# A transformer block on one core: transposes before scaling, 256-byte buffer pitches, later gate sums and 128-row rotary scores

## The chip, the core and the metric

The kernel runs on one core of a Trainium2 chip. Its engines work side by side: TensorE (PE) multiplies matrices, and loads its stationary operands with instructions of their own (PEld); VectorE (DVE) and ScalarE (ACT) do elementwise work; GpSimd (POOL) and SyncE (SP) here mostly issue DMAs. Each engine takes its instructions in order, and waits on semaphores for the others. Operands lie in on-chip memory (SBUF), 128 partitions; a matmul writes to one of eight banks of accumulators (PSUM).

The metric is the device time of one execution in microseconds (us). TensorE's clock is granted by a throttle: 1.00 is full speed.

## What is computed

One layer of a hybrid backbone block, for 256 latent tokens and 256 context tokens of width 2048, all in fp32:

```python
h  = rmsnorm(x, g_attn) * (1 + sc1) + sh1          # and hc from the context tokens
cq, ckv, kr, qn, kn, vn, f = split_columns(h @ w_in)
o_mla = blocked_attention(q_m, cat(k_m, k_mc), cat(v_m, v_mc), MLA_SCALE)   # 8 heads, 128 + 64 rotary
o_na  = neighborhood_attention(...)                # 4 heads
o_fn  = fourier_mix(f, w_fnet)
x  = x + gt1 * (cat(o_mla, o_na, o_fn) @ w_out)
h2 = rmsnorm(x, g_ffn) * (1 + sc2) + sh2
x  = x + gt2 * conv_ffn(h2, w_up, conv_w, conv_b, w_down)
return rmsnorm(x, g_final)
```

The six vectors sh1, sc1, gt1, sh2, sc2, gt2 are silu(c) times a matrix of 2048 x 12288, plus a bias; the context tokens have their own sh1 and sc1.

## The kernel before

**Limbs.** An fp32 operand is held as two numbers of the faster type float32r: a high limb H, and L = value - H. A product of two such operands is three matmuls (`mm3`, lines 108 to 112): H by H, H by L, L by H. Weights come from HBM as raw fp32 tiles of up to 128 x 2048 (SP's queue, `emit_dma`), and `split` makes their limbs: ACT copies to H (line 123), DVE subtracts (line 124). `take(key, i)` (line 181) hands out quarter i of a weight tile and makes limbs ahead of use by `look` quarters, into six `hl` buffers of 4096 bytes per partition.

**Buffers.** Tiles of a tag share that tag's buffers, each as large as the tag's largest tile; tags lie one behind the other. `b8` has 16 buffers. Its largest tile is `h2`, [128, 2, 4, 258] fp32, so the pitch is 8256 bytes; `hx`, `hc`, `act`, `mix`, `hn`, `xT` and the raw weights, of 8192 bytes, lie in it too. `wm2` (4 buffers of 4096 bytes), `acc` (3), `hl` (6), `b1` and `b2` are other tags.

**Stages.** The work on PE, in order:

1. Start. The four tiles of x and context (128 tokens each) are loaded; ACT squares and sums each (line 299), `rstd` gives the inverse root (DVE, POOL), DVE scales x (line 301), and 64 transposes with the identity matrix from `small` turn them into `xT` (line 364).
2. First stage, sixteen rounds. Round g computes sh1 and sc1 for 128 columns (`mod1_mm`, 16 fp32 matmuls of 32 columns of the array, line 318, on 2 MB of `wm1`), transposes the result and makes `hx` and `hc`, the limbs of h (`mod1_h`). `g1` multiplies 128 rows of h by seven column tiles of `wA`, one round behind: four tiles ahead of `mod1_h` and three after it (G1_CUT).
3. V, B and neighbourhood attention, Fourier mixing, latent attention. `mla_scores` makes 128 x 512 scores per head and block: three matmuls on 128 rows, and three on the 64 rotary rows of that head.
4. `wo_unit`: the output projection, then x2, its transposes and h2.
5. Up projection: the first eight pairs on h2 with 258 columns (`up_mm`), the others on `hn` (`up_mm2`, lines 834 and 835: H by H and L in one matmul of 512 columns taken from two places, then L by H with 256 columns). Down projection in four chunks on `act`.

**The other modulation vectors.** The 128 tiles of `wm2` (512 KB each, POOL's queue) are streamed beside all this. `paced` counts matmul columns and calls `fill` at a rate per stage (RATES): one sum that is due, one accumulation on DVE (lines 234 and 236, 128 x 1024), three tiles behind the load (M2_LAG), and one more load. After sixteen tiles a block ends; a gate block's sum is split into limbs, and at the next `fill` PE sums it over the partitions (lines 270 and 271).

The scheduler that lays out each engine's order follows the program, but may pull ready work forward; `tc.issue_after(ins)` holds instructions behind `ins` on its engine.

Of the kernel before, what the change touches and what calls it, by code (L numbers as in the profile page):

```python
# [25 lines left out]
M2_LAG = 3  # L26
CQ_AT = (3, 4, 5)
N_A, G1_CUT = 7, 4
# [4 lines left out]
LOOK_O = 4  # L33
RATES = dict(V=0.647, B=0.336, NA=0.237, F=0.135, FN=0.464, MLA=0.292, O=0.226, UP=0.132, DN=0.428)
# [18 lines left out]
def block_kernel(ctx: ExitStack, tc: tile.TileContext, a, out):  # L53
# [13 lines left out]
    def b8(shape, dt=F32, s="b8"):  # L67
        return sp.tile(shape, dt, tag="b8", bufs=16, name=nm(s))
# [27 lines left out]
    dve.memset(mhalf, -0.5)  # L96
    cs = sp.tile([P, KT, 32], F32, tag="acc", bufs=3, name="cs")
# [10 lines left out]
    def mm3(ps, lH, lL, rH, rL, first, last, skip=False):  # L108
        pe.matmul(ps, lH, rH, start=first, stop=False, skip_group_check=skip)  # L109
        pe.matmul(ps, lH, rL, start=False, stop=False, skip_group_check=skip)  # L110
        pe.matmul(ps, lL, rH, start=False, stop=last, skip_group_check=skip)  # L111
        paced(3 * rH.shape[-1])

# [48 lines left out]
    def quarter(key):  # L162
        if key in kept:
            return b8([P, 2, 512], F32R, s="hk")
        return sp.tile([P, 2, 512], F32R, tag="hl", bufs=6, name=nm("hl"))

    def emit_dma(upto):
        while st[0] <= min(upto, len(order) - 1):
# [4 lines left out]
            last_dma[0] = sync.dma_start(raw[:, :w], a[name][idx]).ins  # L173
# [6 lines left out]

    def take(key, i):

        n = quarters.index((key, i))
        while st[1] <= min(n + look[0], len(quarters) - 1):
            k, q = quarters[st[1]]
            if st[1] > n and order[order.index(k) - 1][0] == "m" and q == 0:
                break
            emit_dma(order.index(k) + ahead[0])
            o, hs = (896 * (q // 2) + 512 * (q % 2), 512 - 128 * (q % 2)) if k[0] == "A" else (
                q * src[k[0]][1] // 4, src[k[0]][1] // 4)  # L190
            t = quarter(k)
# [17 lines left out]
    m2 = {"dma": 0, "acc": 0, "t": {}, "due": None}  # L209
# [31 lines left out]
    def m2_end(blk, acc):  # L241

        if KIND[blk // 2] != "g":
            m2["due"] = (blk, acc)
            return
        lim = []
        for h in range(2):
            hl = sp.tile([P, 2, 512], F32R, tag="acc", bufs=3, name=nm("acl"))
            split(hl[:, 0, :], hl[:, 1, :], acc[:, h * 512 : (h + 1) * 512])
            lim.append(hl)  # L250
        m2["due"] = (blk, lim)

    def m2_sum():
        if m2["due"] is None:
# [13 lines left out]
        for h in range(2):  # L268
            ps = bank()
            pe.matmul(ps, ones_r, v[h][:, 0, :], start=True, stop=False)  # L270
            pe.matmul(ps, ones_r, v[h][:, 1, :], start=False, stop=True)
# [9 lines left out]
    def fill_to(n):  # L281
        while m2["acc"] < n or m2["due"]:
            fill()


    xT = [b8([P, 4, 512], s="xT") for _ in range(4)]
    ssx = const.tile([P, 4], F32, name="ssx")
    rx = const.tile([P, 4], F32, name="rx")
    xt = []
    for t in range(4):  # L290
        x_ = b8([P, D], s="x")
        sync.dma_start(x_, (a["x"] if t < 2 else a["ctx"])[(t % 2) * P : (t % 2 + 1) * P, :])
        xt.append(x_)
        if t == 0:
            act.dma_start(sm, a["small"])
    act.dma_start(rope, a["rope"])
    for t in range(4):
        junk = b8([P, D], s="junk")
        act.activation(junk, xt[t], AF.Square, accum_out=ssx[:, t : t + 1])
        rstd(rx[:, t : t + 1], ssx[:, t : t + 1], D)  # L300
        dve.tensor_scalar(xt[t], xt[t], rx[:, t : t + 1], None, ALU.mult)
    act.activation(c1, smv("c1"), AF.Silu)
# [8 lines left out]
    def mod1_mm(g):  # L311

        for q in range(2):
            w = raw_tile(("m", g, q), 6)
            w = w.rearrange("p (k n) -> p k n", k=8)
            for k in range(8):
                r = 32 * (k % 4)
                pe.matmul(ms[r : r + 32, 0:256], cs[:, 8 * q + k, :], w[:, k, :], start=(q == 0 and k < 4),  # L318
                          stop=(q == 1 and k >= 4), tile_position=(0, r))
        sb = b1(s="part")  # L320
        act.copy(sb, ms[:, 0:256])
        return sb

    def mod1_h(kt, sb):
        for s in range(2):
            pe.transpose(ms[:, 256 + s * P : 256 + (s + 1) * P], sb[:, s * P : (s + 1) * P], ident)
        t = tiny(4, "mt")
        tv = t.rearrange("p (s j) -> p s j", s=2)
        quarters_ = ms[:, 256:512].rearrange("p (s r c) -> p s c r", s=2, r=4)[:, :, 0:2, :]
        dve.tensor_reduce(tv, quarters_, AX.X, ALU.add)  # L330
        dve.tensor_tensor(tv, tv, bm1[:, kt], ALU.add)
        dve.scalar_tensor_tensor(tv[:, 1], tv[:, 1], 1.0, ga[:, kt], ALU.add, ALU.mult)
        m = kt // 4
        if hx[m] is None:
            hx[m] = b8([P, 2, 4, SEQ], F32R, s="hx")
            hc[m] = b8([P, 2, 4, SEQ], F32R, s="hc")
        for j, hh in enumerate((hx, hc)):
# [4 lines left out]
            dve.tensor_scalar(h32, xs, A, B, ALU.mult, ALU.add)  # L342
# [704 lines left out]
```

## Time and profile before

| | us |
|---|---|
| three runs | 1276.1, 1278.97, 1280.82; median 1278.97 |
| profiled execution: device time | 1279.01 |
| its span, first to last instruction | 1277.2 |
| PE, DVE, ACT busy | 1243.7, 978.6, 699.0 |
| mean granted clock | 0.997 |

A row of the profile gives the line, engine and operation of an instruction, its tiles as out<-in, and its shape; in the order of time it begins with start and duration, and ends with the idle time before it and what ended that. Matmuls are pipelined: one of 512 columns lasts 0.39 us and the next starts 0.23 us after it. So for PE the steps from start to start are read, not the durations. PEld overlaps PE.

### The profile page before, as it was taken

How to read it: one execution, taken by the hardware profiler on the slowest of the kernel's cores; microseconds unless marked ns; L12 is line 12 of the kernel's file. 1: busy time of each engine (PE TensorE's matmuls, PEld its weight loads, DVE VectorE, ACT ScalarE, POOL GpSimd, SP SyncE). 2: the span in 40 equal slices, each digit the busy share in tenths (PEclk: the TensorE clock that was granted, in tenths of full speed). 3: DMA queues.
4: the chain of work that ended last, by engine and by line, in shares of the span. 5: the costliest groups of instructions: out<-in, count | busy, mean ns of one | idle time of the engine just before them, and what ended most of it. 6: DMA issues, size and time to landing. Idle time of an engine off the chain costs nothing.

```text
span 1277.2 us, 19956 instructions
## 1 busy us (share of the span) xinstructions
PE 1243.7 (97%) x7536; PEld 1069.2 (84%) x7536; DVE 978.6 (77%) x1757; ACT 699.0 (55%) x1343; POOL 111.5 (9%) x177
## 2 busy tenths in 40 slices
PE   5999999999999999999999999999999999999996
PEld 4888879898787888999988878888888888888885
DVE  5444588999989788899989975777766677777785
ACT  5333323765555555576666544666654566556663
POOL 0000121111111002200121500000000000000000
PEclk9999999999999999999999999999999999999999
DMA  9998689677756977754767857544455645564531
GB/s 387 419 397 327 223 305 323 231 243 249 258 194 232 368 294 270 261 227 165 286 226 253 320 204 264 212 162 169 165 198 180 249 165 183 184 227 165 172 125 66
DMA packets 53648, 304.81 MB, mean 239 GB/s; under 512 B 6064, under 2 KB 7216, under 8 KB 26800
## 3 DMA queue, kind: packets, MB, share of 16 engines
q1 hardware_dynamic: 34256, 234.37, 49.7%
q0 software_dynamic: 18432, 67.12, 15.5%
q10 hardware_dynamic: 864, 2.05, 0.4%
q8 instruction: 59, 0.97, 0.3%
q14 instruction: 37, 0.30, 0.1%
HBM read 301.42 MB, written 2.10 MB: 238 GB/s over the span
## 4 chain that ended last, share of the span: by engine, by line
PE 90%; DMA 3%; DVE 3%; issue 1%; ACT 1%; POOL 0%; DVEq 0%; ACTq 0%; POOLq 0%
PE ps L834 21%; PE ps L109 16%; PE ps L110 15%; PE ps L111 15%; PE ps L835 11%; DMA wm<-in_wm_dram 3%; PE g L109 2%; PE ms L318 2%; PE g L110 2%; PE g L111 2%; DVE acc L236 1%; DVE hl L124 1%; PE ps L493 1%; PE ps L364 1%; DMA sm<-in_small_dram 1%
## 5 line engine op out<-in xcount | busy, mean ns | idle before, releaser
L123 ACT CAST hl<-raw 128x512 fp32r<-128x512 f32 (+2 forms) x732 | 444.0, 611 | 359.8 <-PE ps L111 191.1
L124 DVE TENSOR_TENSOR hl<-raw,hl 128x512 fp32r<-128x512 f32 (+2 forms) x732 | 485.8, 677 | 172.6 <-ACT hl L123 166.4
L834 PE MATMUL ps<-hn,hl 128*128 128x512 f32 x1152 | 404.3, 395 | 0.0
L835 PE MATMUL ps<-hn,hl 128*128 128x256 f32 x1152 | 323.4, 281 | 0.0
L834 PEld LDWEIGHTS ps<-hn,hl 128*128 128x128 f32 x1152 | 216.4, 188 | 51.2
L835 PEld LDWEIGHTS ps<-hn,hl 128*128 128x128 f32 x1152 | 217.1, 188 | 0.2
L236 DVE SCALAR_TENSOR_TENSOR acc<-wm,c,acc 128x1024 f32<-128x1024 f32 x120 | 153.6, 1280 | 8.7 <-DMA wm<-in_wm_dram 8.4
L110 PE MATMUL ps<-hl,act 128*128 128x512 f32 x344 | 135.7, 394 | 0.5 <-DVE hl L124 0.5
L109 PE MATMUL ps<-hl,act 128*128 128x512 f32 x344 | 135.2, 393 | 0.0
L111 PE MATMUL ps<-hl,act 128*128 128x512 f32 x344 | 135.2, 393 | 0.0
L221 POOL DMA_DIRECT2D wm<-in_wm_dram x128 | 68.3, 534 | 310.7 <-DVE acc L236 233.8
L110 PEld LDWEIGHTS ps<-hl,act 128*128 128x128 f32 x344 | 64.7, 188 | 15.9 <-DVE hl L124 1.5
L109 PEld LDWEIGHTS ps<-hl,act 128*128 128x128 f32 x344 | 64.6, 188 | 14.9
L111 PEld LDWEIGHTS ps<-hl,act 128*128 128x128 f32 x344 | 64.7, 188 | 14.6
L109 PE MATMUL ps<-h,hl 128*128 128x258 f32 x256 | 72.5, 283 | 0.0
L111 PE MATMUL ps<-h,hl 128*128 128x258 f32 x256 | 72.1, 282 | 0.0
L110 PE MATMUL ps<-h,hl 128*128 128x258 f32 x256 | 72.1, 282 | 0.0
L216 POOL COPY hold<-hl 128x1 f32<-128x1 f32 x36 | 36.0, 999 | 286.7 <-DVE hl L124 286.7
L109 PE MATMUL ps<-hl,mix 128*128 128x512 f32 x128 | 50.5, 394 | 0.0
L110 PE MATMUL ps<-hl,mix 128*128 128x512 f32 x128 | 50.1, 391 | 0.0
L111 PE MATMUL ps<-hl,mix 128*128 128x512 f32 x128 | 49.9, 390 | 0.0
L855 ACT ACTIVATE cv<-ps,sm 128x256 f32<-128x256 f32 x88 | 49.4, 564 | 0.5
(282 smaller groups left out, 2143.2 us busy)
## 6 DMA issues: line engine op xcount, KB each, us to landing
raw<-in_wup_dram SPq DMA_DIRECT2D x88, 1024.0 KB, 5.1
wm<-in_wm_dram POOLq DMA_DIRECT2D x128, 512.0 KB, 5.1
raw<-in_wdn_dram SPq DMA_DIRECT2D x44, 1024.0 KB, 4.9
raw<-in_wm_dram SPq DMA_DIRECT2D x32, 1024.0 KB, 14.4
raw<-in_wo_dram SPq DMA_DIRECT2D x16, 1024.0 KB, 9.9
raw<-in_wB_dram SPq DMA_DIRECT2D x10, 1024.0 KB, 7.4
raw<-in_wA_dram SPq DMA_DIRECT2D x8, 896.0 KB, 14.5
x<-in_x_dram SPq DMA_DIRECT2D x4, 1024.0 KB, 8.8
```

Of the source, the lines that this page charges most:

```text
L109: pe.matmul(ps, lH, rH, start=first, stop=False, skip_group_check=skip)
L110: pe.matmul(ps, lH, rL, start=False, stop=False, skip_group_check=skip)
L111: pe.matmul(ps, lL, rH, start=False, stop=last, skip_group_check=skip)
L123: act.copy(H, src)
L124: return dve.tensor_tensor(L, src, H.bitcast(F32), ALU.subtract).ins
L216: hold = pool.tensor_copy(tiny(1, "hold"), recent[0][:, 1, 0:1].bitcast(F32)).ins
L221: pool.dma_start(w, a["wm2"][blk * 16 + kt])
L236: dve.scalar_tensor_tensor(m2["a"], w, c1[:, kt : kt + 1], m2["a"], ALU.mult, ALU.add)
L318: pe.matmul(ms[r : r + 32, 0:256], cs[:, 8 * q + k, :], w[:, k, :], start=(q == 0 and k < 4), stop=(q == 1 and k >= 4), tile_position=(0, r))
L834: pe.matmul(ps, w[:, 0, k * P : (k + 1) * P], h[:, :, k, :], start=kt == 0, stop=False, skip_group_check=True)
L835: pe.matmul(ps[:, :SEQ], w[:, 1, k * P : (k + 1) * P], h[:, 0, k, :], start=False, stop=kt == KT - 1, skip_group_check=True)
L855: act.activation(t, ps[:, :SEQ], AF.Identity, bias=c[:, 3:4], scale=c[:, 1:2])
```

## The change

Seven things:

- Transposes work on unscaled x, half a tile at a time, with an identity matrix `idt` that POOL makes; the inverse roots are spread to all partitions as `rxb` by one matmul, and each `mod1_h` multiplies its 128 x 512 of `xT` by it. The x tiles are loaded in halves, the first round's weights between them, `small` and `rope` later.
- In the first stage `a_limbs` makes the limbs of `wA` one round ahead of `g1`, with orders fixed by `issue_after`; G1_CUT is 2. From round 5 on (M2_FROM) fills run there too, at the rate A; the rates V, B and NA are lower.
- Limbs are made 1024 columns at a time, into three buffers of 8192 bytes; `up_mm` goes by halves.
- A gate sum comes SUM_LAG = 6 fills later, except where `fill_to` asks for it at once.
- `qr_limbs` puts H of a head's 64 rotary rows into one half of the partitions and L into the other; scores use two matmuls on 128 rows against krH and krL, which hold the rotary key twice.
- `h8`, four buffers with a pitch of 8448 bytes, takes x, hx, h2, M, f, kh and some of `act`; `b8` has twelve, with a pitch of 8192. h2 has rows of 264 elements; `hn` holds H and L of a row side by side, so line 834's operand is 512 adjoining columns.
- The constants grow by 512 bytes (`idt`).

```diff
-N_A, G1_CUT = 7, 4
+SUM_LAG = 6
+N_A, G1_CUT = 7, 2
-LOOK_O = 4
-RATES = dict(V=0.647, B=0.336, NA=0.237, F=0.135, ...)
+M2_FROM = 5
+LOOK_O = 3
+RATES = dict(A=0.18, V=0.55, B=0.3, NA=0.21, F=0.135, ...)
...
     def b8(shape, dt=F32, s="b8"):
-        return sp.tile(shape, dt, tag="b8", bufs=16, name=nm(s))
+        return sp.tile(shape, dt, tag="b8", bufs=12, name=nm(s))
+    def h8(shape, dt=F32, s="h8"):
+        return sp.tile(shape, dt, tag="h8", bufs=4, name=nm(s))
...
+    idt = const.tile([P, P], F32, name="idt")
+    pool.affine_select(idt, ones, [[1, P]], ALU.is_equal, 0.0, base=0, channel_multiplier=-1)
...
-        return sp.tile([P, 2, 512], F32R, tag="hl", bufs=6, name=nm("hl"))
+        return sp.tile([P, 2, 1024], F32R, tag="hl", bufs=3, name=nm("hl"))
...
-        n = quarters.index((key, i))
-        while st[1] <= min(n + look[0], len(quarters) - 1):
+        n = 2 * half_tiles.index((key, i // 2)) + i % 2
+        while 2 * st[1] <= n + look[0] and st[1] < len(half_tiles):
...
-    def m2_sum():
-        if m2["due"] is None:
+        H, L = [sp.tile([P, 1024], F32R, tag="acc", bufs=3, name=nm("acl")) for _ in range(2)]
+        split(H, L, acc)
+        m2["due"], m2["age"] = (blk, (H, L)), 0
+    def m2_sum(now=False):
+        m2["age"] += 1
+        if m2["due"] is None or not (now or m2["age"] > SUM_LAG):
             return
...
+    def x_in(ts):
+        for t in ts:
+            for h in range(2):
+                junk = sp.tile([P, 1024], F32, tag="acc", bufs=3, name=nm("junk"))
+                last = act.activation(junk, xt[t][:, h * 1024 : (h + 1) * 1024], AF.Square, accum_out=...).ins
+                for m in (2 * h, 2 * h + 1):
+                    ps = bank()
+                    for k in range(4):
+                        kt = 4 * m + k
+                        pe.transpose(ps[:, k * P : (k + 1) * P], xt[t][:, kt * P : (kt + 1) * P], idt)
+                    copied = dve.tensor_copy(xT[m][:, :, t * P : (t + 1) * P], ps.rearrange("p (k q) -> p k q", k=4)).ins
...
+    def x_rms():
...
+        rstd(rx, sst, D)
+        dgs = b2(s="dgx")
+        r = dve.tensor_tensor(dgs.rearrange("p (t q) -> p t q", t=4), ...)
...
+            x_made.append(pe.matmul(ps, ones, dgs, start=True, stop=True).ins)
+        x_made[0] = act.copy(rxb, ps).ins
...
+            dve.tensor_tensor(xk, xk, rxb, ALU.mult)
...
+    def a_limbs(kt, made):
+        k, h = ("A", kt // 2), kt % 2
...
+        with tc.issue_after(made):
+            act.copy(t[:, 0, :896], v)
+        def low():
+            with tc.issue_after(hmade[-1]):
+                last_split[0] = dve.tensor_tensor(t[:, 1, :896], v, t[:, 0, :896].bitcast(F32), ALU.subtract).ins
...
+    x_in(range(2))
+    sb0 = mod1_mm(0)
+    x_in(range(2, 4))
+    x_rms()
     for g in range(KT):
+        if g == 0:
+            mod1_h(0, sb0)
+            continue
+        if g == 1:
+            g1(0, range(0, 4))
...
+        if g == M2_FROM:
+            pace[0] = RATES["A"]
         sb = mod1_mm(g)
-        if g:
-            g1(g - 1, range(0, G1_CUT))
+        low = a_limbs(g, parts[-1])
+        n = 5 if g == 1 else G1_CUT
+        g1(g - 1, range(4 if g == 1 else 0, n))
         mod1_h(g, sb)
-        if g:
-            g1(g - 1, range(G1_CUT, N_A))
+        low()
+        g1(g - 1, range(n, N_A))
...
+    def qr_limbs(q):
+        def limbs(src):
+            for i, hs in enumerate(halves):
+                act.copy(q[hs, i, 2, :], src[hs])
+            for i, hs in enumerate(halves):
+                dve.tensor_tensor(q[halves[1 - i], i, 2, :], src[hs], q[hs, i, 2, :].bitcast(F32), ALU.subtract)
+        return limbs
...
-            hs = slice(64 * i, 64 * i + 64)
-            mm3(ps, q[hs, 0, 2, qs], q[hs, 1, 2, qs], krH[hs, :], krL[hs, :], False, True)
+            pe.matmul(ps, q[:, i, 2, qs], krH, start=False, stop=False)
+            pe.matmul(ps, q[:, i, 2, qs], krL, start=False, stop=True)
...
-    h2 = [b8([P, 2, 4, SEQ + 2], F32R, s="h2") for _ in range(4)]
+    h2 = [h8([P, 2, 4, SEQ + 8], F32R, s="h2") for _ in range(4)]
...
-        hn.append(b8([P, 2, 4, SEQ], F32R, s="hn"))
+        hn.append(b8([P, 4, 2, SEQ], F32R, s="hn"))
...
-                pe.matmul(ps, w[:, 0, k * P : (k + 1) * P], h[:, :, k, :], start=kt == 0, stop=False, skip_group_check=True)
+                pe.matmul(ps, w[:, 0, k * P : (k + 1) * P], h[:, k].rearrange("p s n -> p (s n)"), start=kt == 0, stop=False, skip_group_check=True)
```

More of the change, by code (lines that the diff above doesn't have):

```diff
@@ L110, in mm3 @@
         pe.matmul(ps, lH, rL, start=False, stop=False, skip_group_check=skip)
-        pe.matmul(ps, lL, rH, start=False, stop=last, skip_group_check=skip)
+        ins = pe.matmul(ps, lL, rH, start=False, stop=last, skip_group_check=skip).ins
         paced(3 * rH.shape[-1])
+        return ins
     def paced(n):
@@ L208, in block_kernel @@
     M2 = [(blk, kt) for blk in (0, 1, 4, 5, 2, 3, 6, 7) for kt in range(KT)]
-    m2 = {"dma": 0, "acc": 0, "t": {}, "due": None}
+    m2 = {"dma": 0, "acc": 0, "t": {}, "due": None, "age": 0}
     def m2_dma(n):
@@ L243, in m2_end @@
         if KIND[blk // 2] != "g":
-            m2["due"] = (blk, acc)
+            m2["due"], m2["age"] = (blk, acc), SUM_LAG
             return
[L246 to L251, printed above, removed]
-    def m2_sum():
-        if m2["due"] is None:
+        H, L = [sp.tile([P, 1024], F32R, tag="acc", bufs=3, name=nm("acl")) for _ in range(2)]
[4 more added lines that the diff above has]
+        if m2["due"] is None or not (now or m2["age"] > SUM_LAG):
             return
@@ L293, in block_kernel @@
         xt.append(x_)
[L294 to L302, printed above, removed]
+        if t == 1:
+            emit_dma(order.index(("m", 0, 1)))
@@ new lines, in block_kernel @@
+    emit_dma(order.index(("m", 1, 1)))
+    hmade, hx_made, g1_last, m_mm, x_made, parts = [], [], [], [], [], []
+    def x_in(ts):
+        for t in ts:
+            for h in range(2):
+                junk = sp.tile([P, 1024], F32, tag="acc", bufs=3, name=nm("junk"))
+                last = act.activation(junk, xt[t][:, h * 1024 : (h + 1) * 1024], AF.Square,
+                                      accum_out=ssx[:, 2 * t + h : 2 * t + h + 1]).ins
+                for m in (2 * h, 2 * h + 1):
[4 more added lines that the diff above has]
+                    copied = dve.tensor_copy(xT[m][:, :, t * P : (t + 1) * P], ps.rearrange("p (k q) -> p k q", k=4)).ins
+        x_made[:] = [last, copied]
+        if t == 3:
+            with tc.issue_after(last):
+                act.dma_start(sm, a["small"])
@@ L424, in block_kernel, with rope_T @@
     krL = const.tile([P, 512], F32R, name="krL")
-    def rope_T(ps, H, L):
+    halves = [slice(0, 64), slice(64, 128)]
+    def rope_T(ps, limbs):
         sw, r = b1(s="sw"), b1(s="rr")
@@ L578, in fn_m @@
         w = fn["w"]
-        M = fn["M"] = b8([P, 2, 2, 512], F32R, s="M")
+        M = fn["M"] = h8([P, 2, 2, 512], F32R, s="M")
         for i in range(2):
```

179 lines of the change are left out of this document (110 added, 69 removed).

## The prediction

> **What bounds the kernel now.** I read the page first, then the chain that ended last, then the busy times by stage, and last TensorE in order of time wherever a stage leaves it idle.
>
> ```profile
> span 1277.2 us, 19956 instructions
> PE 90%; DMA 3%; DVE 3%; issue 1%; ACT 1%; POOL 0%; DVEq 0%; ACTq 0%; POOLq 0%
> 31.00:148.00 117.00, 114.52 (x1152) 97.09 (x1145) 50.41 (x140) 39.96 (x82) 1.83 (x6) 1.00 0.89 347
> 148.00:190.00 42.00, 38.99 (x161) 30.91 (x160) 33.87 (x39) 10.72 (x19) 11.08 (x21) 0.96 0.86 303
> 306.00:441.00 135.00, 135.00 (x735) 109.46 (x734) 118.53 (x222) 73.71 (x157) 20.63 (x38) 1.00 0.70 246
> 531.00:640.00 109.00, 109.00 (x848) 105.86 (x848) 103.74 (x204) 76.93 (x153) 10.79 (x16) 1.00 0.63 229
> ```
>
> The stage rows give stretch, length, busy time of PE, PEld, DVE, ACT and POOL, granted clock, DMA share and GB/s. TensorE is the bound nearly everywhere: 90% of the chain, no idle time in the long stretches. So a change pays in three ways only: fewer matmuls, shorter steps from one matmul to the next, or the removal of the few places where PE stands still: the start, the first stage (31 to 148) and the second (148 to 190, where the clock, too, is below 1).
>
> **Rotary scores.** One block of scores of one head:
>
> ```profile
> 335.43 0.40 PE L109 MATMUL ps<-kh,qh 128*128 128x512 f32 x1
> 336.55 0.39 PE L110 MATMUL ps<-krL,qh 64*128 64x512 f32 x1
> 337.11 0.50 PE L109 MATMUL ps<-kh,qh 128*128 128x512 f32 x1
> ```
>
> Starts, not durations, count, since matmuls overlap. Six matmuls take 337.11 - 335.43 = 1.68 us: three of 128 rows, three of 64. After: five of 128 rows, at the 0.233 that the full ones take beside them (below, 341.12 to 344.85) 1.15 at most. There are 8 heads x 2 blocks = 16: 16 x 0.53 = **-8.5 us**. The halved limb writes (two ACT and two DVE instructions instead of one each, four times) lie beside matmuls. What is late next is DVE, 118.5 of 135 us busy here; those 16 x 3 matmuls no longer call `paced`, which takes three accumulations of 1.28 out of the stage, so about 116 of 126, 92%. The stretch 531 to 640 has DVE at 95% and PE without a gap, so I count nothing, with 6 us (the shortfall if DVE could only run at the 88% of now) as the bound.
>
> **Gate sums.** In the second stage PE waits for the limbs of a gate block that has just been finished:
>
> ```profile
> 180.30:183.35 3.05, 0.17 (x1) 0.00 (x1) 2.70 (x4) 0.67 (x2) 0.95 (x2) 1.00 0.93 318
> 183.60:187.00 3.40, 3.27 (x8) 2.34 (x8) 3.40 (x6) 0.74 (x2) 0.54 (x1) 0.50 0.82 305
> 183.35 0.60 PE L270 MATMUL ps<-acl,ones_r 128*128 128x512 f32 x1 [2.88 <-ACT acl L123]
> ```
>
> 3.05 us idle, and behind it 3.40 at half clock, worth half of that: 4.75. With SUM_LAG the sum comes at the seventh `fill` after the block, some ten us later, its limbs long made. The next block's accumulator needs one of three `acc` buffers, and the limbs hold only two. **-4.7 us**. The last sums, called with `now`, gain nothing.
> The Trainium skill (TensorE: Matmul & The Clock Gate, What's actually happening) says that an idle window of about 3.4 us brings the array to half rate; here 3.05 us did, with half rate for 3.40.
>
> **First stage.**
>
> ```profile
> 0.00:5.00 5.00, 0.00 (x0) 0.00 (x0) 0.67 (x3) 0.00 (x0) 0.20 (x4) 1.00 0.61 213
> 15.00:20.00 5.00, 5.00 (x26) 5.00 (x25) 4.27 (x7) 3.67 (x7) 1.10 (x2) 1.00 1.01 420
> 9.56 1.90 ACT junk L299 x2
> 13.66 10.15 PE ps L364 x64
> 23.74 1.93 PE L318 MATMUL ms<-raw,cs 128*32 128x256 f32 x32
> 31.33 0.74 PE L109 MATMUL g<-hx,hl 128*128 128x256 f32 x4
> 42.80:50.00 7.20, 7.20 (x77) 1.00 1.01 419
> 57.31 1.91 PE ms L318 x32
> 87.54 1.91 PE ms L318 x32
> ```
>
> Now nothing starts on PE before 13.66: identity matrix (with `small`), squares, scaling, transposes, in a row. After, transposes need only a half of x and an identity made on chip. But DMA runs full at 0.42 MB/us from about 2.5 us on (213 GB/s x 5 us = 1.07 MB by 5 us), and x (4.2 MB) with the first modulation weights (2.1 MB) ends at 2.5 + 6.3/0.42 = 17.5. From there: the sums and the power, 4.1 as now from squares to transposes (9.56 to 13.66), then 5.7 as now from the end of the first modulation matmuls (25.67) to the first `g1` (31.33): 27.3, 4.0 earlier than now. By 31.33 two and a half modulation groups are done, at 27.3 only one: 1.5 x 1.93 = 2.9 come back. So -1.1. PE stands still between 20 and 27 but for some small work, so by the rows at 183.60 it starts `g1` at half clock: 3.4 to 6.8 us of it, +1.7 to +3.4; I take +2.5. A full round takes 7.20; four rounds from 57.31 to 87.54 take 30.23, 1.4 over 28.8, lost where `hx` and the limbs come late, and so three times: with limbs one round ahead and the order fixed by `issue_after`, -4.2. Sum **-2.8 us**; bounds -8 (no cold start, data as early as it lands) and +6 (the chain at the start 4 us longer, no stall removed).
> Nine fills (14 x 768 columns x 0.427 ns x 0.18 = 0.83 a round, from round 5 on, twelve rounds) come in here: 0.83 x 0.52 MB on POOL's queue beside 2.56 MB of weights a round, 3.0 MB or 7.1 us of DMA for a round of 7.2. Queued behind each accumulation on DVE is the next `hx`. It holds, narrowly (rival 3). Elsewhere the fills are fewer by as many, where PE bounds: nothing.
>
> **Aligned buffers.** Four tiles of activations in one loop of the down projection, 24 matmuls each, and then others:
>
> ```profile
> 711.50 0.39 PE L109 MATMUL ps<-hl,act 128*128 128x512 f32 x1
> 716.94 0.39 PE L109 MATMUL ps<-hl,act 128*128 128x512 f32 x1
> 722.43 0.40 PE L109 MATMUL ps<-hl,act 128*128 128x512 f32 x1
> 728.03 0.39 PE L109 MATMUL ps<-hl,act 128*128 128x512 f32 x1
> 733.60 0.39 PE L109 MATMUL ps<-hl,act 128*128 128x512 f32 x1
> 341.12 0.40 PE L109 MATMUL ps<-hl,kvH 128*128 128x512 f32 x1
> 344.85 0.39 PE L110 MATMUL ps<-hl,kvH 128*128 128x512 f32 x1
> 676.94 0.40 PE L834 MATMUL ps<-hn,hl 128*128 128x512 f32 x1
> 682.56 0.40 PE L834 MATMUL ps<-hn,hl 128*128 128x512 f32 x1
> 546.45 0.28 PE L109 MATMUL ps<-h,hl 128*128 128x258 f32 x1
> 552.21 0.28 PE L109 MATMUL ps<-h,hl 128*128 128x258 f32 x1
> 219.67 0.28 PE L109 MATMUL ps<-hx,hl 128*128 128x256 f32 x1
> 222.50 0.28 PE L109 MATMUL ps<-hx,hl 128*128 128x256 f32 x1
> 223.75 0.28 PE L111 MATMUL ps<-hx,hl 128*128 128x256 f32 x1
> 306.86 0.28 PE L109 MATMUL ps<-cq,hl 128*128 128x256 f32 x1
> 311.04 0.28 PE L111 MATMUL ps<-cq,hl 128*128 128x256 f32 x1
> ```
>
> The steps of the four tiles are 226.7, 228.8, 233.3 and 232.1 ns (5.44, 5.49, 5.60 and 5.57 us by 24). Their buffers differ: `b8` has a pitch of 8256 bytes (from `h2`), so their starts are 32, 224, 96 and 160 modulo 256, while the weight limbs `hl` start at 32. A step is shortest where both agree. After, pitches are 8192 and 8448, the constants grow by 512 bytes, and all these buffers start at 32 modulo 256. So I set each 512-wide matmul to 226.7: `act` 3 x 344 at a mean of 230.2, -3.6; some 480 with `hx`, `hc`, `kv` (341.12 to 344.85: 16 steps, 233.1), -3.1; half of `mix`'s tiles start there already, so 384 x 1.05, -0.4.
> For 256 columns agreement does not help: `cq`, at 32, takes 4.18/35 = 119.4; `hx` takes 113.6 in its buffer at 224 (222.50 to 223.75, 11 steps) and 117.9 in the two before it (219.67 to 222.50, 24 steps): over four buffers 116.9. About 1250 such steps (`g1` 672, projections 576) grow by 2.5: +3.1.
> The pair of lines 834 and 835 takes 5.62/16 = 351.2; after it reads 512 adjoining columns (226.7) and 256 (119.4), 346.1: 1152 x 5.1 = -5.8. The 768 of 258 columns (5.76/48 = 120.0) get rows of 1056 bytes, which no row shows; between 258/256 of 113.6 and of 119.4, middle 117.4: -2.0. Sum **-11.8 us**. Bounds: -24 (all at the best steps seen: pairs at 226.7 + 113.6, 258 columns at 114.5, no loss at 256) and +5 (pairs at 233.3 + 119.4, 512 columns as now).
> The Trainium skill (TensorE: Matmul & The Clock Gate, Wait — 56ns, not 53.3ns?) gives a warm step as columns over 2.4 GHz plus 2.5 ns, so 215.8 for 512, with no address in it, and SBUF — State Buffer (SBUF: two separate sides) has PE's port never wait on anyone. By that rule the term would be 0; the four tiles contradict it, 226.7 to 233.3.
>
> **Limbs 1024 columns at a time.** The same columns in half as many instructions:
>
> ```profile
> L123 ACT CAST hl<-raw 128x512 fp32r<-128x512 f32 x684 | 423.0, 621 | 347.3 <-PE ps L111 184.2 <-PE ps L835 98.6 <-DVE hl L124 40.4
> L236 DVE SCALAR_TENSOR_TENSOR acc<-wm,c,acc 128x1024 f32<-128x1024 f32 x120 | 153.6, 1280 | 8.7 <-DMA wm<-in_wm_dram 8.4
> ```
>
> A half costs at most 2 x 0.62 on ACT and 1.28 on DVE (the 1024-wide row), 2.5 us, and is consumed in 2.8 (12 matmuls at 0.23) with three buffers: hidden by the half before it. **0**; where that cover is gone it is rival 2. At nothing go, too, the identity made by POOL (one instruction on an engine that is 0.20 of the first 5 us busy), `small` and `rope` loaded later (0.5 MB between weights that are not yet due, first used in round 1 and after), `up_mm` in halves (same matmuls), and the sixteen multiplications by `rxb` (half the 1024-wide row, 0.64 each, on a DVE busy 50 of 117 us).
>
> **Sum.** -8.5 - 4.7 - 2.8 - 11.8 = -27.8. The profiled run took 1279.0 (span 1277.2 and 1.8 around it), the median is 1278.97: **1251.2 us**.
>
> **Rivals.** (1) Not the start modulo 256 sets the step, but something that the four tiles share with it (which other buffer is read or written meanwhile), and the new layout moves nothing: the last term is 0, 1263. For it: no row has a pitch of 8192 or 1056. Against it: the weights rotate through their buffers under each tile, and its step stays.
> This is the time that the rule of the Trainium skill's two pages would give.
> (2) Coarser limbs stall the attention stage. `take4` holds two of three buffers for a whole key, so the second half of the next key starts when the first buffer comes free: up to 2.5 plus one queued accumulation, 1.28, less the 2 us that matmuls of both ends cover, 1.8 late, for 10 to 14 keys: +18 to +25, 1269 to 1276, say 1272. For it: DVE at 88%. Against it: other matmuls lie between most keys.
> (3) Slower: accumulations in the first stage wait for their weights. In the second stage DVE does:
>
> ```profile
> 173.09 1.28 DVE L236 SCALAR_TENSOR_TENSOR acc<-wm,c,acc 128x1024 f32<-128x1024 f32 x1 [3.34 <-DMA wm<-in_wm_dram]
> ```
>
> In the first stage `hx` is queued behind it and PE behind `hx`, each time at the price of 180.30 to 187.00, 4.75: eleven rounds give +52, 1304; from seven rounds on the kernel is slower. It begins when a load takes longer than the three fills of M2_LAG, 26 us at 0.83 a round. Against it: the waits of the second stage came with three fills in 4.6 us of matmuls (rate 0.647), a sixth of that.
> (4) More: no cold start (-2.5) and pairs at their best (-6.7): 1242.
>
> **Chances.** A difference under 0.5%, 6.4 us, can't be told from none. Forecast 0.57 (1245 to 1260), (1) 0.14, (2) 0.12, (3) 0.06, (4) 0.11. Faster: 0.57 + 0.14 + 0.11 and half of (2), 0.88; same: the other half, 0.06; slower 0.06. The range 1239 to 1270 takes in some of the bounds at the start beyond (4) and leaves out (3), the outer half of (2) and the end of (4).
>
> **What would show it.** Scores: five 128-row matmuls in 1.15 us. Steps: `act` tiles all at 226.7, pairs near 346, `cq` and `hx` alike at 119.4; unequal tiles would refute the term. No idle at a gate sum before the last stage and clock 1.00 there. First `g1` near 27, rounds of 7.2, the second stage's matmuls some 2.5 earlier. PE waiting for `hl` in the attention stage, or DVE for `wm` in the first, would make the prediction wrong.

## The result, and the profile after

| | before | after |
|---|---|---|
| median of the runs shown with the result, us | 1277.92 (4 runs) | 1267.49 (1266.92 to 1270.93, 4 runs) |
| profiled execution, us | 1279.01 | 1270.93 |
| its span, us | 1277.2 | 1268.9 |

The ratio is 0.9912, with a 95% interval of 0.9895 to 0.9929: 10.4 us less by the medians, 8.1 by the two profiled executions. Faster, as forecast, but by much less than 27.8. The profiled execution is the slowest of the four and has the lowest granted clock of them, 0.990 against 0.992 to 0.994, so the losses read from it below are in all some 3 us larger than those of the median. The page of the kernel after has:

```profile
span 1268.9 us, 18984 instructions
PE 91%; DMA 4%; DVE 2%; POOL 1%; ACT 1%; issue 0%; SPq 0%; DVEq 0%; POOLq 0%; ACTq 0%
```

TensorE still carries the chain, and DMA's share of it has grown from 3% to 4%. The busy times by stage (columns as before):

```profile
33.00:145.00 112.00, 112.00 (x1161) 96.00 (x1160) 62.02 (x143) 36.62 (x63) 6.84 (x14) 1.00 0.99 395
148.00:190.00 42.00, 41.77 (x186) 34.31 (x185) 35.15 (x33) 11.64 (x15) 10.03 (x19) 1.00 0.82 279
190.00:280.00 90.00, 87.06 (x694) 84.41 (x693) 76.24 (x118) 48.75 (x86) 13.16 (x21) 1.00 0.73 252
280.00:309.24 29.24, 26.58 (x118) 21.43 (x117) 20.78 (x27) 12.97 (x17) 1.58 (x3) 0.94 0.72 247
312.66:421.50 108.84, 108.81 (x618) 94.50 (x618) 103.73 (x176) 64.48 (x122) 16.42 (x31) 1.00 0.65 222
```

The first two stages have lost their idle time. The third and the fourth row show idle time of 2.9 us (1.4 in that stage before) and 2.7 us (none before), and the fourth a clock below 1. TensorE in order of time:

```profile
27.67 0.58 PE L117 MATMUL g<-hx,hl 128*128 128x256 f32 x1 [1.89 <-ACT hx L408]
52.04 0.42 PE L374 MATMUL ms<-raw,cs 128*32 128x256 f32 x4
125.19 0.41 PE L374 MATMUL ms<-raw,cs 128*32 128x256 f32 x2
177.94 0.39 PE L290 MATMUL ps<-acl,ones_r 128*128 128x512 f32 x1
337.67 0.39 PE L117 MATMUL ps<-kh,qh 128*128 128x512 f32 x1
338.82 0.39 PE L117 MATMUL ps<-kh,qh 128*128 128x512 f32 x1
562.45 0.28 PE L117 MATMUL ps<-h,hl 128*128 128x258 f32 x1
568.23 0.28 PE L117 MATMUL ps<-h,hl 128*128 128x258 f32 x1
790.51 0.39 PE L938 MATMUL ps<-hn,hl 128*128 128x512 f32 x1
796.15 0.40 PE L938 MATMUL ps<-hn,hl 128*128 128x512 f32 x1
926.18 0.40 PE L117 MATMUL ps<-hl,act 128*128 128x512 f32 x1
931.63 0.39 PE L117 MATMUL ps<-hl,act 128*128 128x512 f32 x1
937.07 0.39 PE L117 MATMUL ps<-hl,act 128*128 128x512 f32 x1
942.51 0.39 PE L117 MATMUL ps<-hl,act 128*128 128x512 f32 x1
```

The first `g1` starts at 27.67. Ten rounds take 125.19 - 52.04 = 73.15, 7.31 each, and none of them is more than 0.1 longer than another. The gate sum of the second stage starts without a wait. A block of scores takes 338.82 - 337.67 = 1.15. The tiles of `act` take 5.44 or 5.45 us by 24 matmuls, 226.8 ns each. The pair of lines 938 and 939 (834 and 835 before) takes 5.64/16 = 352.5 ns (351.8 on the mean of the stage), and a matmul of 258 columns 5.78/48 = 120.4 (120.3 on the mean).

Put on the stages, by the starts of TensorE's last (or first) matmul of each in the two traces, the difference and the forecast's terms stand thus (us):

| stretch | before | after | difference | forecast |
|---|---|---|---|---|
| to the first `g1` | 31.33 | 27.67 | -3.7 | -4.0 |
| first stage, `g1` | 113.87 | 116.96 | +3.1 | +2.9 (modulations, cold clock, 256-wide steps, less the stalls) |
| second stage (V) | 50.42 | 44.87 | -5.6 | -5.9 |
| B and neighbourhood attention | 86.15 | 89.61 | +3.5 | +1.4 |
| Fourier projection | 23.02 | 29.23 | +6.2 | -0.6 |
| latent attention, to the last score | 123.40 | 113.31 | -10.1 | -9.7 |
| output projection | 93.38 | 92.91 | -0.5 | -0.4 |
| up projection, 258 columns | 93.51 | 93.97 | +0.5 | -2.0 |
| up projection on `hn`, down projection | 652.10 | 650.70 | -1.4 | -9.4 |

So nearly all of the shortfall lies in four rows: neighbourhood attention, the Fourier projection, the 258 columns, and the last. Part of it is idle time. These are ACT and PE in the Fourier projection, and DVE and PE early in the down projection:

```profile
289.14 0.84 ACT L132 CAST cw<-dft 128x768 fp32r<-128x768 f32 x1 [2.90 <-DMA dft<-in_dft_dram]
290.82 2.94 ACT L132 CAST hl<-raw 128x1024 fp32r<-128x1024 f32 x3
294.57 0.50 PE L118 MATMUL ps<-hl,hx 128*128 128x512 f32 x1 [1.92 <-DVE hl L133]
722.65 1.28 DVE L258 SCALAR_TENSOR_TENSOR acc<-wm,c,acc 128x1024 f32<-128x1024 f32 x1 [2.44 <-DMA wm<-in_wm_dram]
725.13 0.50 PE L118 MATMUL ps<-hl,act 128*128 128x512 f32 x1 [1.93 <-DVE hl L133]
```

ACT waits 2.90 us for the Fourier matrices `dft`; the casts of the next three halves of weights are queued behind, and PE runs dry. At 722 DVE waits for a tile of `wm2`, with the low limb of the next half behind it. After each of the two the clock is half for 3.41 us (from 295.59 and from 725.67 in the clock's records). Two more things lie at the end of the Fourier projection:

```profile
306.08 1.84 PE L280 MATMUL ps<-ones_r,acc 128*128 128x2 f32 x16
309.24:312.66 3.42, 3.42 (x13) 2.93 (x12) 2.38 (x7) 1.81 (x4) 1.34 (x1) 0.50 0.30 117
```

The sixteen matmuls of 2 columns, which sum a block over the partitions, take 1.7 us; in the kernel before the first of them started at 313.9, in latent attention, so they have only moved from that row to this one. Right behind them the clock is half once more, which costs 1.7 us in latent attention. Of the Fourier row's 6.2 us, then, 2.7 are idle time, 1.7 the half clock from 295.59, and 1.7 these sums.

### The profile page after: what moved, and what is told of

Read it like the earlier page. It is cut to its first block, busy times and chain, and to the rows that moved or that the text cites. A ratio compares the mean times of both kernels' runs of the same rounds, so it can differ in the third digit from the quotient of the medians.

```text
span 1268.9 us, 18984 instructions
## 1 busy us (share of the span) xinstructions
PE 1237.4 (98%) x7522; PEld 1076.2 (85%) x7522; DVE 956.5 (75%) x1408; ACT 634.1 (50%) x976; POOL 109.9 (9%) x175
## 3 DMA queue, kind: packets, MB, share of 16 engines
q10 hardware_dynamic: 864, 2.05, 0.5%
## 4 chain that ended last, share of the span: by engine, by line
PE 91%; DMA 4%; DVE 2%; POOL 1%; ACT 1%; issue 0%; SPq 0%; DVEq 0%; POOLq 0%; ACTq 0%
PE ps L938 21%; PE ps L118 16%; PE ps L117 16%; PE ps L119 16%; PE ps L939 11%; PE g L117 2%; PE ms L374 2%; PE g L118 2%; PE g L119 2%; DMA x<-in_ctx_dram 1%; DMA T<-in_T_dram 1%; PE ps L596 1%; DMA wm<-in_wm_dram 1%; DMA raw<-in_wB_dram 1%; DVE hl L133 1%; DMA dft<-in_dft_dram 1%
## 5 line engine op out<-in xcount | busy, mean ns | idle before, releaser
L133 DVE TENSOR_TENSOR hl<-raw,hl 128x1024 fp32r<-128x1024 f32 (+3 forms) x351 | 421.9, 1205 | 158.7 <-ACT hl L132 157.9
L132 ACT CAST hl<-raw 128x1024 fp32r<-128x1024 f32 (+3 forms) x351 | 363.4, 1036 | 349.9 <-PE ps L119 247.8
L938 PE MATMUL ps<-hn,hl 128*128 128x512 f32 x1152 | 405.5, 397 | 0.0
L258 DVE SCALAR_TENSOR_TENSOR acc<-wm,c,acc 128x1024 f32<-128x1024 f32 x120 | 153.5, 1279 | 9.2 <-DMA wm<-in_wm_dram 8.7
L960 DVE SCALAR_TENSOR_TENSOR cv<-ps,sm,cv 128x255 f32<-128x255 f32 x88 | 42.1, 480 | 20.0 <-ACT cv L959 20.0
L238 POOL COPY hold<-hl 128x1 f32<-128x1 f32 x36 | 34.1, 948 | 233.3 <-DVE hl L133 164.1
L117 PE MATMUL ps<-hl,mix 128*128 128x512 f32 x128 | 50.4, 394 | 0.0
L118 PE MATMUL ps<-hl,mix 128*128 128x512 f32 x128 | 49.9, 390 | 0.0
## 6 DMA issues: line engine op xcount, KB each, us to landing
raw<-in_wV_dram SPq DMA_DIRECT2D x4, 1024.0 KB, 10.4
```

The source lines that it names most:

```text
L132: act.copy(H, src)
L133: return dve.tensor_tensor(L, src, H.bitcast(F32), ALU.subtract).ins
L238: hold = pool.tensor_copy(tiny(1, "hold"), recent[0][:, 1, 0:1].bitcast(F32)).ins
L258: dve.scalar_tensor_tensor(m2["a"], w, c1[:, kt : kt + 1], m2["a"], ALU.mult, ALU.add)
L938: pe.matmul(ps, w[:, 0, k * P : (k + 1) * P], h[:, k].rearrange("p s n -> p (s n)"), start=kt == 0, stop=False, skip_group_check=True)
L960: dve.scalar_tensor_tensor(t[:, 1:], ps[:, : SEQ - 1], c[:, 0:1], t[:, 1:], ALU.mult, ALU.add)
```

## Experiments

Each was timed against the kernel before in the same series, and stands with the ratio to it; the change itself has 0.9912. A difference of 0.0024 between two ratios, some 3 us, is about what two such intervals can tell; what is smaller is read from the traces alone. All kernels compute the whole; e13 adds a product.

### One common start for all buffers

```diff
     c1 = const.tile([P, KT], F32, name="c1")
+    pad = const.tile([P, 8], F32, name="pad")        # e2: [P, 56]
+    dve.memset(pad, 0.0)
```

> The changed kernel with 32 unused bytes more among the constants, so that every buffer behind them starts at 64 instead of 32 modulo 256; nothing else. Theory A (the prediction's: a matmul's step depends on whether its two operands agree modulo 256): they agree as before, 512 columns stay at 227 ns, 256 at 120, the pair of lines 938 and 939 at 352; the time stays near 1267. Theory B (each operand that starts off a multiple of 64 bytes reads one more line of 64 bytes): steps fall by 5 to 13 ns each, 512 columns to 214 to 222, 256 to 107 to 115, the pair to 325 to 340; the time falls by 20 to 45 us.

> As the run before, with 224 bytes, so that every buffer starts at 0 modulo 256. Theory A: 227, 120 and 352 ns, near 1267. Theory B: the same steps as with 32 bytes. Theory C (only multiples of 128 or 256 are free of cost): steps fall here and not with 32 bytes.

Measured: 0.9917 (0.9884 to 0.9949) and 0.9918 (0.9888 to 0.9948). Every step is as in the kernel after: medians 227 for `act`, 120 for `hx`, 235 and 117 for the two matmuls of a pair. Where the buffers start in common does not matter. That it is their agreement modulo 256 that sets the step of matmuls of one width fits all steps seen here, but no run moves one operand alone, so another property of the layout is not excluded.

### Parts alone, on the kernel before

The edits are those of the change: `qr_limbs` and line 770's two matmuls; SUM_LAG with `m2_end` and `m2_sum`; `b8`, `h8`, h2's rows and `hn`.

> The kernel before with the 128-row rotary scores alone. Theory A (the matmuls saved go straight into the time): 16 blocks x 0.53 us = 8.5, plus 1 to 2 us for three accumulations that leave the stage, so 8 to 10 us less than the kernel before, the last score matmul 8 to 10 us earlier. Rival: DVE and ACT of the attention stage take part of it back, 3 to 6 us less.

> The kernel before with the later gate sums alone (and the limbs of a gate block in two tiles of 1024 columns). Theory A: the idle of 3.05 us at the second stage's gate sum and the half clock behind it go, 4.7 to 6 us less, with the stage's end 4.7 to 6 us earlier. Rival: PE then waits elsewhere in that stage for the accumulations, 0 to 2 us less.

> The kernel before with the buffers alone (twelve of 8192 and four of 8448 bytes, rows of 264 elements in h2, H and L of a row side by side in hn). By the prediction's term: 11.8 us less, pairs of matmuls at 346 ns. Theory from the changed kernel's steps: 512-wide steps at 227 (some 6 to 7 us less), 256-wide steps at 120 (3 us more), pairs unchanged at 351 to 352 and 258-wide steps at 120.5: 3 to 4 us less in all.

Measured: 1.0037 (1.0024 to 1.005), 1.0017 (1.0005 to 1.0029) and 1.0039 (1.0027 to 1.0052). None of the three pays alone. With the rotary scores alone, the attention stage is 9.5 us shorter, and then PE waits:

```profile
513.36 0.24 PE L260 MATMUL ps<-ones_r,acc 128*128 128x2 f32 x1 [2.91 <-DVE acc L236]
```

and the row of the stretch behind it shows the clock at 0.50:

```profile
514.20:524.40 10.20, 9.46 (x44) 9.05 (x44) 6.85 (x23) 3.49 (x16) 1.55 (x2) 0.50 0.42 143
```

The `fill_to` ahead of the up projection asks for a block of accumulations that is not done: the stage that became shorter had also carried some of them. 2.91 us of waiting, and 10.2 at half clock, worth 5.1. From the last matmul of the output projection to the last of 258 columns it takes 103.4 where the kernel before takes 93.5: what was won is gone. With the sums alone, the second stage is 5.9 shorter, and the next one 6.8 longer:

```profile
220.81 0.50 PE L110 MATMUL ps<-knH,qn 128*128 128x512 f32 x1 [2.22 <-ACT qn L124]
224.27 0.50 PE L112 MATMUL ps<-knH,qn 128*128 128x512 f32 x1 [1.78 <-DVE qn L125]
...
222.60 1.28 DVE L237 SCALAR_TENSOR_TENSOR acc<-wm,c,acc 128x1024 f32<-128x1024 f32 x1
```

On DVE an accumulation stands just ahead of the limb `qn` that the second one waits for: the accumulations come at the same columns of work, and with PE earlier they meet the next stage. With the buffers alone, all tiles of `act` run at 226.7 ns and the pairs stay at 352, but the first stage is 9 us longer. Some 1.8 of this are the 256-wide steps of `g1` (119.5 ns for 116.8), and only one group of modulations comes ahead of the first `g1` (groups start at 25.3, 34.0 and 37.2; before at 23.7, 26.9 and 30.3). That the raw weights have four buffers fewer at the start is the likely reason for the latter, not shown. From the end of the second stage on it takes 1069.3 against 1071.6, 2.3 less.

### One part left out of the change

```diff
-M2_FROM = 5                                  # e9, with V=0.647, B=0.336, NA=0.237
+M2_FROM = 99
-SUM_LAG = 6                                  # e10
+SUM_LAG = 0
```

e11 and e12 put the old rotary scores and the old buffers back.

> The changed kernel without fills in the first stage, and with the old rates of V, B and NA: the one part that gives the stream of accumulations a lead. Theory A (the other parts pay only because the stream is ahead by nine to fifteen accumulations; alone, the time saved on PE comes back where a gate sum or an accumulation is waited for, as at 513 us with the rotary scores alone): 6 to 14 us slower than the changed kernel, with waits in the neighbourhood stage and before the up projection. Rival (the fills in the first stage only cost, by DMA taken from the weights): the same or up to 3 us faster.

> The changed kernel with gate sums at the next fill, as before. Theory A: an idle of 2 to 3 us and a half clock behind it come back at each gate sum that meets busy PE, in the second stage and in the down projection: 3 to 6 us slower than the changed kernel. Rival (with the stream ahead, the waits only move, as they did with the sums alone): within 2 us.

> The changed kernel with the old rotary scores. Theory A (here the stream is ahead and nothing waits before the up projection, so the stage's 10 us count in full): 8 to 11 us slower than the changed kernel. Rival (part of it comes back later here too, as all of it did with the rotary scores alone): 0 to 5 us slower.

> The changed kernel with sixteen buffers of 8256 bytes, rows of 258 elements in h2 and the old hn. By the prediction's term: 11.8 us slower than the changed kernel. Theory from the steps seen: 512-wide steps go back to 226 to 233 (some 6 us), 256-wide ones from 120 to 117 (3 us the other way), pairs stay: 2 to 5 us slower.

| left out | ratio to before | 95% | against the change, x 1279 us |
|---|---|---|---|
| fills in the first stage | 0.9982 | 0.9966 to 0.9998 | +9.0 |
| lag of the sums | 0.9950 | 0.9931 to 0.9969 | +4.9 |
| rotary scores | 0.9988 | 0.9976 to 0.9999 | +9.7 |
| buffers | 0.9988 | 0.9974 to 1.0001 | +9.7 |

Here the first three parts are worth about what their stages show. The first row explains why: without the lead that the fills of the first stage give, the wait ahead of the up projection is back, and without the lag the gate sum's (e9, then e10):

```profile
512.61 0.24 PE L280 MATMUL ps<-ones_r,acc 128*128 128x2 f32 x1 [3.90 <-DVE acc L258]
```

```profile
171.61 0.80 PE L290 MATMUL ps<-acl,ones_r 128*128 128x512 f32 x1 [3.85 <-ACT acl L132]
```

Leaving the buffers out cost more than the 2 to 5 expected. The steps of three tiles of `act` in that run:

```profile
925.30 0.40 PE L115 MATMUL ps<-hl,act 128*128 128x512 f32 x1
942.07 0.40 PE L115 MATMUL ps<-hl,act 128*128 128x512 f32 x1
```

16.77/72 = 232.9 ns, against 226.8. The old buffers bring back the old steps tile by tile: in the first part of the down projection (700 to 790 us) they are about 229, 227, 233 and 233 ns in turn, a cycle of four like the one in the kernel before; in the part from which the rows are, all tiles are slow, and so they are in the kernel before (232.0 to 233.3 ns from 934 to 1000 us). Over the down projection the steps sum to 244.7 us against 239.5 (stalls taken out), the output projection takes 1.1 more, and the pairs sum to 405.5 against 405.3, no difference. The other 3 us or so are not settled: the profiled executions of the two kernels are only 2.8 us apart (1273.76 and 1270.93), that of e12 lying 4.1 us below the median of its kernel and that of the change 3.4 above.

### Limbs, and the late Fourier matrices

e4 issues the limbs of `dft` in the third quarter of the Fourier projection; e8 makes all limbs 512 columns at a time, into six buffers.

```diff
-    def proj_N(kind, toks):
+    def proj_N(kind, toks, mid=None):
...
+                if mid and (q, k) == (2, 2):
+                    mid()
```

> The changed kernel, with the two limb splits of the Fourier matrices issued in the third quarter of the F projection instead of ahead of it, so that ACT makes two halves of F's limbs before it waits for that load. If that wait (2.9 us on ACT with three halves queued behind it) is what stops PE at 291 and 294 us, these gaps of 0.9 and 2.1 us go, and with them the 3.4 us at half clock: -4 to -6 us. If the F weights' own limbs or loads are late, the gaps stay and the time is near 1267.

> The changed kernel with limbs made 512 columns at a time into six buffers, as before. Theory A (the coarse limbs lengthen what stands in the queues behind a late load): the stall before the Fourier stage's end (2.97 us idle and 3.41 at half clock) and the one early in the down projection (2.08 idle, 3.41 at half clock) go, 5 to 9 us less than the changed kernel, 1258 to 1262. Rival B (the loads themselves come late, whatever the limbs): the stalls stay, 1266 to 1269. Rival C (limbs two quarters ahead are worse in the first stage): above 1270.

Measured: 0.9888 (0.9856 to 0.9919) and 0.9891 (0.9876 to 0.9906), 3.1 and 2.7 us below the change. The stretch 280 to 305, in the kernel after, e4 and e8:

```profile
280.00:305.00 25.00, 22.34 (x90) 17.56 (x89) 18.26 (x22) 11.84 (x15) 1.06 (x2) 0.93 0.76 263
```

```profile
280.00:305.00 25.00, 25.00 (x122) 20.73 (x120) 21.40 (x26) 13.24 (x18) 1.59 (x3) 1.00 0.68 230
```

```profile
280.00:305.00 25.00, 25.00 (x122) 20.88 (x121) 21.77 (x37) 14.02 (x26) 1.70 (x4) 1.00 0.86 310
```

Either edit removes the idle time and both stretches of half clock; the projection takes 24.4 instead of 29.2. By time alone the two gains are at the edge of what the intervals can tell, and e8's is less than the 5 to 9 us expected. In e4 ACT comes to the load at 290.50, after three more casts of the projection's limbs, and does not wait for it: what stood behind it in ACT's queue was the harm. With 512 columns, three casts stand ahead of it and the wait shrinks to 0.34:

```profile
285.60 1.66 ACT L132 CAST hl<-raw 128x512 fp32r<-128x512 f32 x3
287.60 0.84 ACT L132 CAST cw<-dft 128x768 fp32r<-128x768 f32 x1 [0.34 <-DMA dft<-in_dft_dram]
```

The stall early in the down projection was 1.6 us of idle time in e8, and absent in e3 and e4, whose edits lie elsewhere. So the width of the limbs does not decide it; what does is not shown.

### What keeps the pair at 352 ns

e13 makes the second matmul of a pair as wide as the first. e3, e17 and e18 put four, eight and sixteen 512-wide matmuls ahead of as many 256-wide ones (e17 and e18 on e16, below).

```diff
-                pe.matmul(ps[:, :SEQ], w[:, 1, k * P : (k + 1) * P], h[:, k, 0, :], start=False, ...)
+                pe.matmul(ps, w[:, 1, k * P : (k + 1) * P], h[:, k].rearrange("p s n -> p (s n)"), start=False, ...)
```

> The changed kernel with the second matmul of each pair in the up projection as wide as the first: 512 columns, so that the product of the two low limbs is added. It asks what keeps the pair at 352 ns. Theory A (the mix of two widths): all steps of the stage are then 227, 454 for the pair. Theory B (weights that change with every matmul as the stationary operand, or the tile hn itself): the 512-wide steps stay at 231 to 236 on the mean, 462 to 472 for the pair. The whole kernel is 110 to 135 us slower by the wider matmuls.

> The changed kernel, with the four 512-column matmuls of a quarter first and its four 256-column ones behind them (lines 938 and 939 in two loops). If alternating widths set the pair's 352 ns, the 512s go to 227 and the 256s to 113 to 120, a pair to 340 to 347: -6 to -14 us. If the pair is dear because of what it reads (moving tiles in b8, stationary limbs), it stays at 350 to 353 and the time at 1267.

> The kernel with the three edits and the earlier stream, with eight 512-wide matmuls ahead of eight 256-wide ones instead of four. The homogeneous run has steps of 227 at 512 columns, and 120 is the rule for 256: 346.7 a pair; groups of one give 351.8, groups of four 350.7. Theory A (a change of width disturbs some steps behind it, so fewer changes cost less): 348 to 349.5 a pair, 1.4 to 3 us less. Theory B (widths mixed in whatever order keep the steps off 227): 350 to 351, no gain.

> The same with all sixteen 512-wide matmuls of a tile ahead of its sixteen 256-wide ones, which holds four of six limb buffers at once. Theory A: 347 to 348.5 a pair, 2.5 to 4.5 us less than with groups of four, if the limbs come in time. Theory B: 350 to 351. Rival (the limbs of the next tile then come late): PE idles at the start of each tile, 48 tiles with 0.2 us or more, 5 us more or worse.

Two starts, sixteen pairs apart, in e13:

```profile
811.40 0.39 PE L938 MATMUL ps<-hn,hl 128*128 128x512 f32 x1
818.65 0.39 PE L938 MATMUL ps<-hn,hl 128*128 128x512 f32 x1
```

7.25/32 = 226.6 ns: with one width the same tiles and weights run at the forecast step, so the operands are not to blame. In e18, one tile (sixteen matmuls of line 948, then those of 951):

```profile
790.90 0.40 PE L948 MATMUL ps<-hn,hl 128*128 128x512 f32 x1
792.06 0.61 PE L948 MATMUL ps<-hn,hl 128*128 128x512 f32 x2
794.10 0.61 PE L948 MATMUL ps<-hn,hl 128*128 128x512 f32 x2
794.56 0.28 PE L951 MATMUL ps<-hn,hl 128*128 128x256 f32 x1
794.67 0.40 PE L951 MATMUL ps<-hn,hl 128*128 128x256 f32 x2
```

The first five steps after 256-wide matmuls take 1.16 us, 232 each; the next nine 2.04, 226.7. The first 256-wide step takes 0.11, and the rest 0.120. A change of width back to 512 costs about 27 ns over five steps, and the change to 256 gives 8 of them back. The mean pair falls with the number of changes: 351.8 ns in the kernel after, 350.7 in groups of four, 349.1 of eight, 347.8 of sixteen, as theory A had it. Times: e13 1.0817 (2 runs, wider matmuls), e3 0.9890 (0.9866 to 0.9915), e17 0.9889 (0.9873 to 0.9906), e18 0.9865 (0.9846 to 0.9883). The gain of the larger groups shows in the steps and not in the time. Against e16, from which e17 and e18 differ in the grouping alone, e17 is 0.0023 slower and e18 the same, where theory A had 1.4 to 3 and 2.5 to 4.5 us less than groups of four: e17 met idle time of 3.7 us in neighbourhood attention and 2.9 early in the down projection, and e18 1.8 there, places that their edits don't touch.

### Edits together

e14 takes e3, e4 and e8 together; e15 adds an earlier load of the tables T; e16, instead, begins the last block of accumulations in the up projection.

```diff
         if j < 4:
+            T = na_T(j)                              # e15: the loads out of na_scores
             ps = bank()
...
+        if pace[0] == RATES["UP"]:                   # e16, in up_mm2
+            pace[0] = 0.18
-RATES = dict(..., DN=0.428)
+RATES = dict(..., DN=0.33)
```

> The changed kernel with three edits together: limbs of 512 columns, the limbs of the Fourier matrices in the third quarter of the projection, and the 512-wide matmuls of a quarter ahead of its 256-wide ones. Theory A (three places, each paid for once): the first two remove the same stall of some 5 us, the third gives 1.3, and the stall early in the down projection is 0 to 2 us: 1259 to 1263. Rival (what is saved comes back at the next wait): 1264 to 1268.

> The same three edits, and each head's tables T of the neighbourhood attention issued one projection earlier. Theory A (the waits of 0.9 and 1.6 us at 227 to 232 us are for T, issued 4 to 8 us too late): 1.5 to 3 us less than with the three edits alone, the last projection matmul of the stage by as much earlier. Rival (the tables then take a b2 buffer from the scores before, or push the weights on the queue): no gain or a loss of up to 2 us.

> The same three edits, with the accumulations of the last block begun in the up projection (rate 0.18 there on hn, 0.33 in the down projection). Theory A (the stall early in the down projection is DMA: 16 loads of 512 KB within 27 us beside the weights): fewer loads in that stretch, no idle over 0.5 us there, 0 to 2 us less than with the three edits alone. Rival (DVE in the up projection is short, too): PE idles in the up projection instead, up to 3 us more.

Measured: e14 0.9873 (0.9857 to 0.9890), e15 0.9875 (0.9861 to 0.9890), e16 0.9866 (0.9851 to 0.9881). PE in neighbourhood attention, in e14 and in e15:

```profile
227.99 0.50 PE L117 MATMUL ps<-knH,qn 128*128 128x512 f32 x1 [1.41 <-ACT qn L132]
```

```profile
227.89 0.50 PE L117 MATMUL ps<-knH,qn 128*128 128x512 f32 x1 [1.41 <-ACT qn L132]
```

The tables were not it: the wait is for ACT, which has the softmax of the head before in its queue, and stays. The stretch 690 to 727, in the kernel after, in e16 and in e18:

```profile
690.00:727.00 37.00, 35.07 (x163) 29.00 (x162) 31.87 (x37) 15.70 (x20) 15.01 (x20) 0.98 0.82 294
```

```profile
690.00:727.00 37.00, 37.00 (x170) 30.81 (x169) 33.74 (x50) 19.37 (x34) 8.37 (x10) 1.00 0.71 247
```

```profile
690.00:727.00 37.00, 35.24 (x161) 28.49 (x160) 32.73 (x48) 18.13 (x31) 12.42 (x14) 1.00 0.71 264
```

In e16 the stall is gone, but that the earlier stream removed it is not shown: e18 has the same stream and the same 0.71 of DMA, and 1.76 us of idle time, while e3 and e4 have none with DMA at 0.86. e16 and e18, at 1261.21 and 1260.91 us, are the fastest: 17 us below the kernel before, and 6 below the change by the ratios. From e14 they can't be told apart by time.

## Why the prediction was wrong in size

- **Bound and direction.** Right. TensorE bounds the kernel, and the three ways in which a change can pay were the right ones to look for.
- **Rotary scores, -8.5.** Right: 1.15 us a block, and 10.1 off the stage, the forecast's 9.7 with the 512-wide steps included. It is luck that nothing blurs the row: the sums that left it and the half clock that came in are 1.7 us each. The working took it for certain that PE's time there is the kernel's; it is only while the accumulations keep up (+4.7 alone, -9.7 within the change).
- **Gate sums, -4.7.** Right in the stage, 5.6 for 5.9 with the 512-wide steps; without the lead that the fills of the first stage give, it comes back in the next one (+6.8 in e6, +6.1 in e9).
- **First stage.** Right: 27.67 for 27.3, rounds of 7.31 where 7.2 and 42 steps longer by 2.5 ns give 7.3, no stalls, and half clock at the start, 6.83 us of it, worth 3.4 for the 2.5 forecast. Rival 3, accumulations that wait for weights there, did not come: DMA is at 0.99, and PE has no idle time.
- **Aligned buffers, -11.8: the step that failed.** "after it reads 512 adjoining columns (226.7) and 256 (119.4), 346.1: 1152 x 5.1 = -5.8" adds up steps that were read where one width follows itself. In an alternation they don't hold: 352, whichever buffers the pairs read (352.1 with the old ones, e12), and the pairs sum to +1.2 instead of -5.8. With one width (e13) the forecast's 226.7 is there, and the pair comes to 347.8 when its widths are grouped by sixteen (e18). The middle value of 117.4 for 258 columns failed as well: 120.3, by the rule for 256 that the same paragraph had found, +0.5 instead of -2.0. The other terms held: 226.7 for `act`, 120 for all tiles of 256 columns. Rival 1 fell by e7 and e12, in which the steps of `act` follow the buffers; that the measured 1267 lies nearer to its 1263 than to 1251 is chance. The Trainium skill (TensorE: Matmul & The Clock Gate, Wait — 56ns, not 53.3ns?) gives columns over 2.4 GHz plus 2.5 ns. Here the steady steps are that quotient plus 13.3, at 512 columns (226.7) and at 256 (120).
- **Limbs, 0: failed too.** "hidden by the half before it" holds where only limbs are queued. Behind a load that is late, a queue of wide instructions is long: 2.7 us of idle time and 1.7 for half clock in the Fourier projection, which limbs of 512 columns (e8) or a later wait (e4) remove. Rival 2 named the mechanism, but placed it in latent attention, where PE's idle time is 0.03 us. The working did not look at which other instructions of ACT and DVE wait for a load.
- **The last rows.** Neighbourhood attention lost 2.1 more than its 256-wide steps, 1.5 of it idle time; e15 shows that it isn't the tables' loads, and more is not known. The early down projection has 2.05 us of idle time and 1.7 for half clock, where the kernel before had 1.34 of idle time.
- **Sum.** Of the 19.7 us by which the profiled executions miss the forecast (16.3 by the median), the pairs are 7.0, the Fourier projection 6.8, the 258 columns 2.5, and the two stretches of the point before this one 4.5; the other terms came out 1.1 better than forecast.

## What to carry to other kernels

Read the step from one matmul to the next in the very sequence in which it will run: where widths alternate, neither width keeps the step that it has in a run of its own, and grouping by width gets most of it back. When an engine off the critical path has a stream to finish by fixed points, time saved ahead of such a point can be worth nothing until the stream is ahead, too; so try a part of a change both alone and as the one part left out. Before an instruction is made wider, look for the loads that its queue waits for: what stands behind a late load is late by its own length as well.

## What the runs showed of the hardware

A change of matmul width is felt for five steps: 233, 236, 228, 232 and 231 ns at 512 columns after 256, then 227; and 113, 119, then 120 at 256 after 512 (medians over the tiles of e18).

Half clock does not follow from the length of an idle time alone. 1.93 us at 725 was followed by 3.41 us of it; in e6, 2.22 at 220.81 and 1.78 at 224.27 by none:

```profile
220.81:228.00 7.19, 5.40 (x37) 4.93 (x38) 7.14 (x12) 3.41 (x6) 1.07 (x2) 1.00 1.04 361
```

In the kernel after, half clock begins at 25.94, 295.59, 309.24 and 725.67 us: the distances are 79, 4 and 122 times 3.413. So the windows lie on a grid that runs through the whole execution, and what counts is how an idle time lies in it: of those of e6, 1.85 us lie in one window and 1.74 in the next. Laid on each trace's own grid, all twenty traces agree between 40 and 1245 us. Of some 7000 windows at full clock, sixteen had 1.92 us or more in which TensorE had nothing but matmuls of 2 columns or none at all, and just these were followed by half clock; among the others the longest such time is 1.85. That matmuls of 2 columns count as idle time here is read from the window ahead of 309.24, in which the profile shows PE busy throughout. The Trainium skill (TensorE: Matmul & The Clock Gate, What's actually happening) has the window free-running with 3413 ns; the trace agrees with that. It asks for an idle window of that length; here less than 2 us idle was enough.
